# A hybrid attention block: other latencies in the hand-made order of the tensor engine, and a gate tile in the first head

## The chip, the core and the metric

The kernel runs on one core of a Trainium2 chip. Its engines work side by side, each from its own queue of instructions and in the order of that queue: TensorE (PE in the rows, PEld for its weight loads), VectorE (DVE), ScalarE (ACT), GpSimd (POOL) and SyncE (SP), which here only issues DMAs. The metric is the time of one execution in device microseconds (us), smaller is better; the kernel before takes 1390.83 us, the median of three runs from 1388.82 to 1392.7.

## What is computed

One layer on 512 tokens of width 1024, all in float32. Shortened from the reference:

```python
u = rmsnorm(h, pre_mix_norm)
proj = u @ w_in                       # q, k, v of attention; qkv, z, b, a of the delta rule; 2 gates
o_a = diff_attention(da_q, da_k, da_v, ...)          # 8 heads, softmax1 - lam * softmax2
qkv = silu(causal_depthwise_conv(gdn_qkv, conv_w))
g_q, g_k = l2norm(...), l2norm(...)                  # 8 heads, each for 2 value heads
o_b = gated_delta_rule(g_q, g_k, g_v, log_decay, beta)
o_b = rmsnorm(o_b) * silu(gdn_z)
merged = sigmoid(gate_a) * (o_a @ w_branch_a) + sigmoid(gate_b) * (o_b @ w_branch_b)
h = h + rmsnorm(merged @ w_out)
h = h + rmsnorm(square(relu(rmsnorm(h) @ w_up)) @ w_down)
h = h + rmsnorm((p @ w_ple) * sigmoid(h @ w_ple_gate))
```

The delta rule works on chunks: a triangular matrix is inverted for each chunk, and then a state is carried from chunk to chunk.

## The kernel before

Every large product is a "dense tile": 128 output channels by 512 tokens, with weights and activations split into a high and a low part, so three matmuls for each 128 rows of the weights. A tile of the input projection is 24 matmuls of 128x512 (`dense_steps`); `fill` yields after each pair of them.

Between the prologue and the branch products lies the scheduled section, in which the input projection (filler, in the order of `units`) and the work of the eight heads (chains) share TensorE. A head h has six chains, each a generator that emits a step and then yields:

- A (`gdn_a`): transposes and squares of keys and queries (psk, psq), the products of keys and queries (psx), and the transposed values (psv). One PSUM buffer, tag "a".
- I (`gdn_i`): the inverse of the 16x16 blocks, on VectorE (tiles L, Uq, tmpq), with DMAs through DRAM (ld_d, ud_d) ahead of it and behind it.
- U (`gdn_u`): the inverse is widened to the full block in matmul steps: psY16, psU16, psY, psT and psU, ps6, ps7.
- S (`gdn_s`): the states. For each of four chunks: psS (from the state's halves Sh and Sl), X, psV, vs and vn, psN and psO, and the new state.
- N (done mark "B", `gdn_n`): the norm of the delta rule's output, the transposes psoT, the product zs, and its store to ob_d.
- T (`attn`): differential attention, four blocks of 128 queries: psat (scores), softmax to aw, psaT (transposes), aT, psao, and at the end psaoT.

U, S and N take their PSUM buffers from one pool with two buffers (pool pb, tag "b"), which go round in the order of allocation: an allocation waits until the reader of the one before the last has finished.

What a generator yields is the assumed latency: the number of us of TensorE work that shall stand between this step and the chain's next. `run` keeps a clock that adds the estimated time of the emitted matmuls and nothing else. It emits the first chain in the list whose due time has come, otherwise the next filler pair; with neither it would let the clock jump. So the yields fix the order of TensorE's queue when the program is built. The other engines' queues are ordered by the framework's scheduler by priority (`URGENT`). What is on a queue waits for what stands ahead of it. A chain starts when the marks it names are done: U of head h waits for U of head h-1, A for A of h-1, and so on. After the last head's tiles 16 branch gate tiles follow as filler (`branch_gate`: tanh to gth, stored to g_d).

The names in rows are the program's, with the buffer numbers left out, so psY and psY16 both read psY, and ps6 and ps7 both ps. All matmuls of helper `mm` have line 80.

Of the kernel before, what the change touches and what calls it, by code (L numbers as in the profile page):

```python
# [37 lines left out]
def hybrid_block(ctx, tc, xT, pT, w1, wba, wa, wb, wo, wup, wdn, wple, wpg, vecs, rows, consts, out):  # L38
# [276 lines left out]
    done = set()  # L315
# [202 lines left out]
    def gdn_u(hk):  # L518

        B, U = (st_[hk][n] for n in "BU")  # L520
        Bf = B.rearrange("p i c n -> p (i c) n")
        U4 = U.rearrange("p e (k n) -> p e k n", k=4)
        bq = b0, b1, b2, b3 = [slice(32 * i, 32 * i + 32) for i in range(4)]
        yield 18.0

        T16 = [TT[:, :, 0], TA[:, :, 1], TT[:, :, 1], T3]
        for i in range(4):
            V.transpose(T16[i][bq[i]], U4[bq[i], :, i])
        Y16 = [Ye[:, :, 0], Yx[:, :, 0, :16], Ye[:, :, 1], Yx[:, :, 1, :16]]
        yield 6.0  # L530
        psY16 = pb.tile([128, 8, 16], F32, name="psY16", tag="b")
        for e in range(8):
            for i in range(4):
                mm(psY16[bq[i], e], Bf[:, e, bq[i]], T16[i][:, e, :16])
        for i in range(4):
            if i % 2:
                S.activation(Y16[i][bq[i]], psY16[bq[i]], AF.Copy, scale=nm16[bq[i]])
            else:
                V.tensor_scalar(Y16[i][bq[i]], psY16[bq[i]], nm16[bq[i]], None, op0=mult)
        yield 2.0  # L540
        psU16 = pb.tile([128, 8, 16], F32, name="psU16", tag="b")
        for e in range(8):
            for i in range(4):
                mm(psU16[32 * i:32 * i + 16, e], Y16[i][:, e], U4[:, e, i, 16:])
        for i in range(4):
            (S.copy if i % 2 else V.tensor_copy)(U4[32 * i:32 * i + 16, :, i, 16:], psU16[32 * i:32 * i + 16])
        yield 2.0
        V.transpose(TT[b0, :, 0], U4[b0, :, 0])
        V.transpose(TT[b2, :, 1], U4[b2, :, 2])
        V.transpose(TA[b1, :, 1], U4[b1, :, 1])  # L550
        V.tensor_copy(TA[b0, :, 0], TT[b0, :, 0])
        yield 5.0
        psY = pb.tile([128, 8, 32], F32, name="psY", tag="b")
        for e in range(8):
            mm(psY[b1, e], Bf[:, e, b1], TT[:, e, 0])
            mm(psY[b3, e], Bf[:, e, b3], TT[:, e, 1])
        V.tensor_scalar(Yx[b1, :, 0], psY[b1], -1.0, None, op0=mult)
        S.activation(Yx[b3, :, 1], psY[b3], AF.Copy, scale=-1.0)
        yield 2.0
        psT = pb.tile([128, 8, 32], F32, name="psT", tag="b")  # L560
        for e in range(8):
            mm(psT[b1, e], U[:, e, b1], Yx[:, e, 0])
        V.tensor_copy(TA[b1, :, 0], psT[b1])
        psU = pb.tile([128, 8, 32], F32, name="psU", tag="b")
        for e in range(8):
            mm(psU[b0, e], Yx[:, e, 0], U4[:, e, 1])
            mm(psU[b2, e], Yx[:, e, 1], U4[:, e, 3])
        S.copy(U4[b0, :, 1], psU[b0])
        V.tensor_copy(U4[b2, :, 3], psU[b2])
        yield 2.0  # L570
        ps6 = pb.tile([128, 8, 64], F32, name="ps6", tag="b")
        for e in range(8):
            mm(ps6[64:, e], Bf[:, e, 64:], TA[:, e])
        done.add(("B_read", hk))
        S.activation(Y6[64:], ps6[64:], AF.Copy, scale=-1.0)
        yield 2.0
        ps7 = pb.tile([64, 8, 64], F32, name="ps7", tag="b")
        for e in range(8):
            mm(ps7[:, e], Y6[:, e], U[:, e, 64:128])
        V.tensor_copy(U[:64, :, 64:128], ps7)  # L580
        yield 2.0

    def gdn_s(hk):

# [5 lines left out]
        for c in range(NC):  # L590
            c0 = c * 128
            if c:
                psS = pb.tile([128, 2, 2, 128], F32, name="psS", tag="b")
                ch = slice(c0, c0 + 128)
                for n in range(2):
                    mm(psS[:, n], kqh[:, n, ch], Sh, stop=False)
                    mm(psS[:, n], kql[:, n, ch], Sh, start=False, stop=False)
                    mm(psS[:, n], kqh[:, n, ch], Sl, start=False)
                X = bp.tile([128, 2, 128], F32, name="X")
                qs = bp.tile([128, 2, 128], F32, name="qs")  # L600
                for i in range(2):
                    hv = 2 * hk + i
                    V.scalar_tensor_tensor(X[:, i], in0=psS[:, 0, i], scalar=nbeg[:, c, hv:hv + 1], in1=vb[:, i, c], op0=mult, op1=add)
                for i in range(2):
                    hv = 2 * hk + i
                    S.activation(qs[:, i], psS[:, 1, i], AF.Identity, scale=eg[:, c, hv:hv + 1])
                xs = X
                yield 2.5
            else:
                xs = vb[:, :, 0]  # L610
            psV = pb.tile([128, 2, 128], F32, name="psV", tag="b")
            for i in range(2):
                mm(psV[:, i], U[:, 4 * i + c], xs[:, i])
            if c < NC - 1:
                vs = bp.tile([128, 2, 128], F32, name="vs")
                for i in range(2):
                    V.tensor_scalar(vs[:, i], psV[:, i], edr[:, i, c:c + 1], None, op0=mult)
            vn = bp.tile([128, 2, 128], F32, name="vn")
            S.activation(vn, psV, AF.Identity, scale=r2[:, c:c + 1])
            yield 2.5  # L620
            if c < NC - 1:
                psN = pb.tile([128, 2, 128], F32, name="psN", tag="b")
                mm(psN, kt[:, c], vs)
                Sn = bp.tile([128, 2, 128], F32, name="Sn", bufs=2)
                if c:
                    for i in range(2):
                        hv = 2 * hk + i
                        V.scalar_tensor_tensor(Sn[:, i], in0=St[:, i], scalar=egl[:, c, hv:hv + 1], in1=psN[:, i], op0=mult, op1=add)
                else:
                    V.tensor_copy(Sn, psN)  # L630
                St = Sn
                Sh, Sl = (bp.tile([128, 2, 128], F32R, name=f"S{n}") for n in "hl")
                split(Sh, Sl, St)
            psO = pb.tile([128, 2, 128], F32, name="psO", tag="b")
            for i in range(2):
                mm(psO[:, i], intra[:, i, c], vn[:, i])
            for i in range(2):
                if c:
                    V.tensor_tensor(o[i][:, c], psO[:, i], qs[:, i], op=add)
                else:  # L640
                    V.tensor_copy(o[i][:, c], psO[:, i])
                junk = bp.tile([128, 128], F32, name="bjunk")
                S.activation(junk, o[i][:, c], AF.Square, accum_out=sso[:, i, c:c + 1])
            if c < NC - 1:
                yield 3.0

    def gdn_n(hk):

# [4 lines left out]
        rsqrt(bp, rt.rearrange("p a c -> p (a c)"), sso.rearrange("p a c -> p (a c)"), 2 * NC)  # L653
        for i in range(2):
            V.tensor_tensor(o[i], o[i], bc(rt[:, i], [128, NC, 128], 2), op=mult)
        yield 11.0
        for i in range(2):
            zs = d["zs", i]
            psoT = pb.tile([128, T], F32, name="psoT", tag="b")
# [35 lines left out]
    def attn(h):  # L695
# [13 lines left out]
        for b in range(NC):  # L709
# [18 lines left out]
            V.scalar_tensor_tensor(rr, in0=rr, scalar=st[:, 2:3], in1=nlam, op0=mult, op1=mult)  # L728
            V.tensor_scalar(l2[:, b:b + 1], st[:, 2:3], st[:, 2:3], EPS, op0=mult, op1=mult)
            V.scalar_tensor_tensor(ws[0][:, :n], in0=ws[1][:, :n], scalar=rr, in1=ws[0][:, :n], op0=mult, op1=add)  # L730
            yield 6.0 + 0.5 * b
            psa = pt.tile([128, NC, 128], F32, name="psaT", tag="t")
            for kb in range(b + 1):
                transpose(psa[:, kb], ws[0][:, kb * 128:(kb + 1) * 128])
            aT = apool.tile([128, NC, 128], F32, name="aT", bufs=2)
            S.copy(aT[:, :b + 1], psa[:, :b + 1])
            yield 1.5
            pso = pt.tile([128, 128], F32, name="psao", tag="t")
            for kb in range(b + 1):
                mm(pso, aT[:, kb], vt[:, kb], start=kb == 0, stop=kb == b)  # L740
# [24 lines left out]
    def units():  # L765
        for h in range(-1, 8):
# [6 lines left out]
            if h >= 0:  # L773
                yield gate_tile(h, 0)
                yield gate_tile(h, 1)
            if h < 7:
                yield ak_tile(h + 1)
                yield av_tile(h + 1)
        for n in range(16):
            yield branch_gate(n)  # L780

    done |= {(n, -1) for n in ("kq_read", "B_read", "k_read", "av_read", "B", "T", "A", "I", "U")} | {("B_read", -2)}
    done |= {("v_read", -1, i) for i in range(2)} | {(n, -2) for n in "BT"}
    for h in range(8):
        chains.append([0.0, (("Z", h, 1), ("S", h)), gdn_n, h, ("B", h)])
        chains.append([0.0, (("U", h), ("B", h - 1)), gdn_s, h, ("S", h)])
        chains.append([0.0, (("I", h), ("U", h - 1)), gdn_u, h, ("U", h)])
        chains.append([0.0, (("av", h), ("T", h - 1)), attn, h, ("T", h)])
        chains.append([0.0, (("V", h, 1), ("A", h - 1)), gdn_a, h, ("A", h)])
        chains.append([0.0, (("A", h), ("I", h - 1)), gdn_i, h, ("I", h)])  # L790
    manual = tc.manual_schedule(engines={PE.engine})
    manual.__enter__()
# [308 lines left out]
```

## Time and profile before

| | |
|---|---|
| median of 3 runs | 1390.83 us |
| the profiled execution | 1397.38 us, its span 1395.6 us |
| TensorE busy | 1326.7 us (95% of the span), 8402 matmuls |
| VectorE, ScalarE, GpSimd busy | 838.1, 662.3, 184.5 us |
| mean granted TensorE clock | 0.98 of full |

"Idle before" is the time in which the engine did nothing ahead of an instruction, and the name behind the arrow is what ended it. PEclk is the granted clock of TensorE as a share of full speed. A row of waits gives the total in us, how often, and the longest.

### The profile page before, as it was taken

The numbers are of one execution on the slowest core, as the hardware profiler recorded it, in microseconds if no ns is written. First come the engines' busy times: TensorE is split into PE (matmuls) and PEld (weight loads), VectorE is DVE, ScalarE is ACT, GpSimd is POOL, SyncE is SP. The second block draws the span as 40 slices with busy tenths as digits, with TensorE's granted clock in tenths as the row PEclk, the third lists the DMA queues.
The fourth block names the chain that finished last, engine by engine and source line by source line (L and its number), as shares of the span: only waits on it lengthen the run. The fifth ranks groups of instructions, "written<-read, shape, count | busy, mean of one in ns | idle before, by whom it ended". The sixth has DMA issues, their size and how long they took to land.

```text
span 1395.6 us, 22459 instructions
## 1 busy us (share of the span) xinstructions
PE 1326.7 (95%) x8402; PEld 1107.5 (79%) x8402; DVE 838.1 (60%) x2155; ACT 662.3 (47%) x1363; POOL 184.5 (13%) x193
## 2 busy tenths in 40 slices
PE   6989999999999999999999999999999999999986
PEld 4867787787777778878888888898888888888985
DVE  6867688777778768776653534368343224433575
ACT  5556575767667476766453412254232223223241
POOL 3111111101111111110000000003320002210341
PEclk9989999999999999999999999999999999999998
DMA  7466655655665566655354743351232233223321
GB/s 249 134 153 132 154 122 135 157 150 126 162 158 139 134 134 166 149 135 143 117 185 167 249 143 113 101 186 46 67 100 91 91 94 102 91 91 108 112 84 61
DMA packets 91117, 182.58 MB, mean 131 GB/s; under 512 B 33632, under 2 KB 40160, under 8 KB 91008
## 3 DMA queue, kind: packets, MB, share of 16 engines
q1 hardware_dynamic: 81648, 147.07, 33.6%
q0 software_dynamic: 9360, 34.08, 13.2%
q8 instruction: 66, 1.08, 0.3%
q14 instruction: 43, 0.35, 0.1%
HBM read 130.19 MB, written 16.84 MB: 105 GB/s over the span
## 4 chain that ended last, share of the span: by engine, by line
PE 73%; DVE 14%; DMA 6%; ACT 3%; SPq 2%; issue 2%; POOL 0%; DVEq 0%; ACTq 0%; POOLq 0%
PE ps L80 64%; DMA dt<-gcr_d 2%; DVE Uq L507 1%; SPq L474 1%; PE psat L80 1%; DVE tmpq L506 1%; DVE h L881 1%; PE psao L80 1%; DMA L<-ld_d 1%; DVE ht L880 1%; DVE acc L372 1%; DMA U<-ud_d 1%; PE psS L80 1%; PE psx L80 1%; DVE nw_t L93 1%
## 5 line engine op out<-in xcount | busy, mean ns | idle before, releaser
L80 PE MATMUL ps<-u_hi,whi 128*128 128x512 f32 (+1 forms) x952 | 385.0, 405 | 0.0
L80 PE MATMUL ps<-u_lo,whi 128*128 128x512 f32 (+1 forms) x952 | 374.8, 395 | 0.0
L80 PE MATMUL ps<-u_hi,wlo 128*128 128x512 f32 (+1 forms) x952 | 250.1, 396 | 0.0
L98 ACT CAST whi<-raw 128x1024 fp32r<-128x1024 f32 (+1 forms) x116 | 116.4, 1005 | 265.4 <-PE ps L80 258.5
L80 PEld LDWEIGHTS ps<-u_hi,whi 128*128 128x128 f32 x952 | 183.2, 192 | 35.4
L80 PEld LDWEIGHTS ps<-u_lo,whi 128*128 128x128 f32 x952 | 183.4, 193 | 33.9
L99 DVE TENSOR_TENSOR wlo<-raw,whi 128x1024 fp32r<-128x1024 f32 x106 | 130.1, 1227 | 126.5 <-PE ps L80 104.2
L80 PEld LDWEIGHTS ps<-u_hi,wlo 128*128 128x128 f32 x952 | 172.6, 189 | 33.7 <-issue 0.2
L117 POOL DMA_DIRECT2D wlo<-raw x65 | 56.2, 864 | 424.5 <-ACT wlo L116 224.6
L80 PE MATMUL ps<-hid_hi,whi 128*128 128x512 f32 x224 | 88.5, 395 | 0.0
L80 PE MATMUL ps<-hid_lo,whi 128*128 128x512 f32 x224 | 88.4, 394 | 0.0
L80 PE MATMUL ps<-brl,whi 128*128 128x512 f32 x208 | 82.1, 394 | 0.0
L80 PE MATMUL ps<-brh,whi 128*128 128x512 f32 x208 | 82.0, 395 | 0.0
L372 DVE SCALAR_TENSOR_TENSOR acc<-ps,cw,acc 128x511 f32<-128x511 f32 (+2 forms) x96 | 71.3, 743 | 8.5 <-ACT acc L369 7.7
L115 ACT CAST whi<-raw 128x1024 fp32r<-128x1024 f32 x65 | 68.0, 1046 | 17.3 <-PE ps L80 17.0
L116 ACT ACTIVATE wlo<-whi 128x1024 fp32r<-128x1024 f32 x65 | 68.6, 1056 | 0.3
L942 POOL TENSOR_TENSOR mr<-mr 128x512 f32<-128x512 f32 (+1 forms) x37 | 39.5, 1070 | 217.9 <-ACT hid_hi L941 217.2
L940 DVE SCALAR_TENSOR_TENSOR mr<-ps,r 128x512 f32<-128x512 f32 (+1 forms) x37 | 22.9, 619 | 74.4 <-PE ps L80 70.7
L80 PE MATMUL ps<-hid_hi,wlo 128*128 128x512 f32 x224 | 56.9, 395 | 0.0
L80 PE MATMUL ps<-brh,wlo 128*128 128x512 f32 x208 | 52.6, 395 | 0.0
L80 PEld LDWEIGHTS ps<-hid_lo,whi 128*128 128x128 f32 x224 | 42.1, 188 | 10.3
L80 PEld LDWEIGHTS ps<-hid_hi,wlo 128*128 128x128 f32 x224 | 42.0, 188 | 10.2
(334 smaller groups left out, 2425.4 us busy)
## 6 DMA issues: line engine op xcount, KB each, us to landing
raw<-w SPq DMA_DIRECT2D x88, 512.0 KB, 3.5
wlo<-raw POOLq DMA_DIRECT2D x65, 512.0 KB, 4.8
raw<-wup SPq DMA_DIRECT2D x32, 512.0 KB, 3.3
raw<-wdn SPq DMA_DIRECT2D x32, 512.0 KB, 3.6
raw<-wb SPq DMA_DIRECT2D x16, 512.0 KB, 3.9
dt<-gcr_d SPq DMA_DIRECT2D x16, 256.0 KB, 5.1
bB<-ber_d SPq DMA_DIRECT2D x16, 256.0 KB, 5.2
ob_d<-zs SPq DMA_DIRECT2D x16, 256.0 KB, 3.0
```

The source lines that it names most:

```text
L80: PE.matmul(ps, lhsT=lhsT, rhs=rhs, start=start, stop=stop, **k)
L93: V.tensor_tensor(t, t, h, op=mult)
L98: S.copy(hi, src)
L99: (eng or V).tensor_tensor(lo, src, hi.bitcast(F32), op=sub)
L115: S.copy(whi, raw)
L116: S.activation(wlo, whi.bitcast(F32), AF.Copy, scale=-1.0)
L117: nc.gpsimd.dma_start(wlo, raw, accum_op=add)
L372: V.scalar_tensor_tensor(acc[:, s:], in0=ps[:, :T - s], scalar=cw[:, j, w:w + 1], in1=acc[:, s:], op0=mult, op1=add)
L474: nc.sync.dma_start(dst, Bf[bs, :, bs])
L506: V.tensor_tensor(tv, bc(L[:, j, j + 1:], [128, m, r], 1), bc(Uq[:, :m, j], [128, m, r], 2), op=mult)
L940: V.scalar_tensor_tensor(r[:, :n], in0=ps[:, :n], scalar=0.0, in1=r2[:, sl], op0=mx, op1=mult)
L942: G.tensor_tensor(r[:, :n], r[:, :n], r[:, :n], op=mult)
```

## The change

Three things change, all in the order of the scheduled section.

1. Assumed latencies: in U the yields behind psY16, psU16, psY, psT with psU, ps6 and ps7 go from 2.0 to 3.0. In S the yield behind psS goes from 2.5 to 3.0, the one behind psV from 2.5 to 3.5, and the one at the end of a chunk from 3.0 to 3.5. In N 11.0 becomes 12.0. In T the softmax's 6.0 + 0.5b becomes 7.0 + 0.5b, and the copy of aT 1.5 becomes 2.5.
2. Branch gate 0 moves from the end of the filler to a place behind head 0's two z gates.
3. A of head h also waits until S of head h-2 is done.

```diff
@@ gdn_u (six yields alike)
-        yield 2.0
+        yield 3.0
@@ gdn_s, behind psV
-            yield 2.5
+            yield 3.5
@@ units
+            if h == 0:
+                yield branch_gate(0)
             if h < 7:
                 yield ak_tile(h + 1)
                 yield av_tile(h + 1)
-        for n in range(16):
+        for n in range(1, 16):
             yield branch_gate(n)
@@ marks and chains
-    done |= {("v_read", -1, i) for i in range(2)} | {(n, -2) for n in "BT"}
+    done |= {("v_read", -1, i) for i in range(2)} | {(n, -2) for n in "BTS"} | {("S", -1)}
-        chains.append([0.0, (("V", h, 1), ("A", h - 1)), gdn_a, h, ("A", h)])
+        chains.append([0.0, (("V", h, 1), ("A", h - 1), ("S", h - 2)), gdn_a, h, ("A", h)])
```

Three places show what this does to the queues. The first is TensorE in the first softmax block of head 0, where psaT is the transpose of the softmax's output aw and psao the product that reads its copy aT; whi and wlo are the weights of filler tiles. The rows with - are before, those with + now.

```order
-L80 MATMUL ps<-u_hi,wlo_866 128x512 x2
+L80 MATMUL ps<-u_hi,wlo_866 128x512 x8
 L80 MATMUL psaT<-C,aw 128x128
-L80 MATMUL ps<-u_hi,wlo_866 128x512 x6
-L80 MATMUL ps<-u_hi,whi_947 128x512
-L80 MATMUL ps<-u_lo,whi_947 128x512
-L80 MATMUL psao<-vt,aT 128x128
```

psaT now stands six filler matmuls later. psao, the last row taken away here, stands twelve filler matmuls behind psaT where it stood eight behind it: ten more than before from the queue's common point.

The second place is ScalarE in head 1's A chain and head 0's third softmax block, before; the squares of psq (junk) are what psx waits for, and aw is the softmax's exponential, which waits for VectorE's maximum st.

```order
L420 COPY kt<-psk 128x512
L373 ACTIVATE vraw_1128<-acc 128x512
L115 CAST whi_1261<-raw_1259 128x1024
L721 ACTIVATE aw,st<-psat,st 128x384 x2
L413 ACTIVATE junk,gss<-psq 128x128
L674 ACTIVATE q_1253<-ps 64x512
```

The same place now:

```order
L420 COPY kt<-psk 128x512
L373 ACTIVATE vraw_1123<-acc 128x512
L115 CAST whi_1241<-raw_1239 128x1024
L743 ACTIVATE ajunk,asso<-oo 128x128
L413 ACTIVATE junk,gss<-psq 128x128 x3
L674 ACTIVATE q_1233<-ps 64x512
L413 ACTIVATE junk,gss<-psq 128x128
L116 ACTIVATE wlo_1242<-whi_1241 128x1024
L674 ACTIVATE q_1234<-ps 64x512
L721 ACTIVATE aw,st<-psat,st 128x384 x2
```

The squares of psq now stand ahead of the softmax's exponentials, and not behind them.

The third place is TensorE at head 1's step psT with psU of the U chain, before; both take a buffer of pool pb.

```order
L80 MATMUL psv<-C,vraw_1955 128x128 x4
L80 MATMUL psT<-Yx,U_349 32x32 x8
L80 MATMUL psU<-U_349,Yx 32x32 x16
L80 MATMUL psaT<-C,aw 128x128 x4
L80 MATMUL ps<-u_hi,wlo_2080 128x512 x6
```

The same place now:

```order
L80 MATMUL ps<-u_hi,whi_2188 128x512
L80 MATMUL ps<-u_lo,whi_2188 128x512
L80 MATMUL psO<-vn,intra 128x128 x2
L80 MATMUL psT<-Yx,U_349 32x32 x8
L80 MATMUL psU<-U_349,Yx 32x32 x16
L80 MATMUL psat<-k_1598,q_1233 128x512
```

psO of head 0's last chunk, also of pool pb, has come to stand straight ahead of psT and psU; psU takes the buffer that psO has just filled.

## Rows read from the trace of the kernel before

**Rows 1.** Stages: length, busy us (instructions) of five engines, granted clock, DMA share, GB/s.
```profile
70.00:665.00 595.00, 562.82 (x4339) 465.06 (x4338) 444.59 (x1434) 384.00 (x895) 83.58 (x86) 0.97 0.61 144
665.00:770.00 105.00, 105.00 (x724) 87.34 (x724) 52.42 (x118) 45.98 (x92) 0.00 (x0) 1.00 0.47 158
```

**Rows 2.** TensorE's waits, 35 to 775 us: total, times, longest.
```profile
PE psV L80 <- DVE X L603: 4.0, 5, 1.1
PE psao L80 <- ACT aT L736: 3.5, 1, 3.5
PE psx L80 <- ACT junk L413: 3.0, 1, 3.0
PE psN L80 <- DVE vs L617: 2.8, 2, 2.3
PE psoT L80 <- DVE zs L662: 2.6, 2, 1.5
PE psN L80 <- DVE tmpq L506: 2.5, 1, 2.5
PE psT L80 <- DVE Yx L557: 2.3, 1, 2.3
PE psaT L80 <- DVE aw L730: 2.1, 1, 2.1
PE psx L80 <- DVE l L729: 1.9, 1, 1.9
PE psS L80 <- ACT Sh L98: 1.6, 2, 1.0
PE psU L80 <- ACT Yx L537: 1.4, 4, 0.8
PE psO L80 <- ACT vn L619: 1.0, 2, 0.8
PE psY L80 <- DVE Sn L628: 0.9, 1, 0.9
PE psoT L80 <- ACT U L546: 0.6, 1, 0.6
...
PE ps L80 <- DVE zs L662: 0.5, 1, 0.5
```

**Rows 3.** Stretches of half clock, first and last of seven; columns as in Rows 1.
```profile
94.10:104.20 10.10, 6.63 (x17) 4.80 (x16) 8.50 (x25) 5.22 (x10) 2.57 (x3) 0.50 0.58 160
...
496.80:500.20 3.40, 3.40 (x12) 2.81 (x10) 2.83 (x9) 2.28 (x7) 0.86 (x1) 0.50 0.84 213
```

**Rows 4.** TensorE in time, at full and at half clock: start, us, instruction.
```profile
66.65 0.39 PE L80 MATMUL ps<-u_hi,whi 128*128 128x512 f32 x1
66.88 0.39 PE L80 MATMUL ps<-u_lo,whi 128*128 128x512 f32 x1
...
94.57 0.63 PE L80 MATMUL ps<-u_hi,whi 128*128 128x512 f32 x1
95.00 0.63 PE L80 MATMUL ps<-u_lo,whi 128*128 128x512 f32 x1
```

**Rows 5.** VectorE and ScalarE in time, three places: columns as Rows 4, then idle before.
```profile
90.22 0.36 DVE L431 SCALAR_TENSOR_TENSOR dt<-dt,gc_t,C 128x128 f32<-128x128 f32 x1 [4.71 <-DMA dt<-gcr_d]
...
98.79 0.26 ACT L736 COPY aT<-psaT 128x128 f32<-128x128 f32 x1
98.95 0.62 ACT L98 CAST kqh<-kq 128x512 fp32r<-128x512 f32 x1
...
121.93 0.43 DVE L528 STREAM_TRANSPOSE TT<-U 32x256 f32<-32x256 f32 x1 [2.80 <-DMA U<-ud_d]
```

**Rows 6.** The branch products and reloads: ns min/median/max, first and last start.
```profile
L80 PE MATMUL ps<-brh,whi x208: 390/394/404, 769.5 to 912.4; 128*128 128x512 f32 x104
L99 DVE TENSOR_TENSOR brl<-ot,brh x12: 1211/1226/1226, 719.9 to 799.8; 128x1024 fp32r<-128x1024 f32 x12
```

**Rows 7.** VectorE's waits for the dt tiles, 70 to 770 us: columns as in Rows 2.
```profile
DVE dt L431 <- DMA dt<-gcr_d: 15.4, 8, 4.7
```

More of the change, by code (lines that the diff above doesn't have):

```diff
@@ L546, in gdn_u @@
             (S.copy if i % 2 else V.tensor_copy)(U4[32 * i:32 * i + 16, :, i, 16:], psU16[32 * i:32 * i + 16])
-        yield 2.0
+        yield 3.0
         V.transpose(TT[b0, :, 0], U4[b0, :, 0])
@@ L558, in gdn_u @@
         S.activation(Yx[b3, :, 1], psY[b3], AF.Copy, scale=-1.0)
-        yield 2.0
+        yield 3.0
         psT = pb.tile([128, 8, 32], F32, name="psT", tag="b")
@@ L569, in gdn_u @@
         V.tensor_copy(U4[b2, :, 3], psU[b2])
-        yield 2.0
+        yield 3.0
         ps6 = pb.tile([128, 8, 64], F32, name="ps6", tag="b")
@@ L575, in gdn_u @@
         S.activation(Y6[64:], ps6[64:], AF.Copy, scale=-1.0)
-        yield 2.0
+        yield 3.0
         ps7 = pb.tile([64, 8, 64], F32, name="ps7", tag="b")
@@ L580, in gdn_u @@
         V.tensor_copy(U[:64, :, 64:128], ps7)
-        yield 2.0
+        yield 3.0
     def gdn_s(hk):
@@ L607, in gdn_s @@
                 xs = X
-                yield 2.5
+                yield 3.0
             else:
@@ L619, in gdn_s @@
             S.activation(vn, psV, AF.Identity, scale=r2[:, c:c + 1])
-            yield 2.5
+            yield 3.5
             if c < NC - 1:
@@ L644, in gdn_s @@
             if c < NC - 1:
-                yield 3.0
+                yield 3.5
     def gdn_n(hk):
@@ L655, in gdn_n @@
             V.tensor_tensor(o[i], o[i], bc(rt[:, i], [128, NC, 128], 2), op=mult)
-        yield 11.0
+        yield 12.0
         for i in range(2):
@@ L730, in attn @@
             V.scalar_tensor_tensor(ws[0][:, :n], in0=ws[1][:, :n], scalar=rr, in1=ws[0][:, :n], op0=mult, op1=add)
-            yield 6.0 + 0.5 * b
+            yield 7.0 + 0.5 * b
             psa = pt.tile([128, NC, 128], F32, name="psaT", tag="t")
@@ L736, in attn @@
             S.copy(aT[:, :b + 1], psa[:, :b + 1])
-            yield 1.5
+            yield 2.5
             pso = pt.tile([128, 128], F32, name="psao", tag="t")
```

## The prediction

> **What bounds the kernel now.** I read the stages first. TensorE has no free time from 665 to 770 us, and the change ends there; what it can touch is the stretch from 70 to 665 us, where TensorE is busy 562.8 of 595.0 us at a mean clock of 0.97 [rows 1]. So 32.2 us of idle time is the first pot. The second is the clock: seven stretches stand at half of full speed (1.2 and not 2.4 GHz), one of 10.1 us and six of about 3.4 us [rows 3]. There two matmuls of 512 columns start 0.43 us apart and not 0.23 [rows 4], so a stretch loses about half its length, 1.6 us for a short one and 5 us for the long one. Both pots together hold some 45 us; work that TensorE does is not changed at all, 8 heads and 16 gates in either order.
>
> The waits of TensorE tell who fills the first pot [rows 2]. They come in four kinds, and the sum below goes by them: (a) psaT and psao in the first softmax block, 2.1 + 3.5 = 5.6 us; (b) steps whose assumed latency is raised, psV, psN, psO, psS, psU and psT, together 15.6 us; (c) steps that found no free buffer of the two in pool pb, psoT behind zs and U, psY behind Sn and ps7 behind zs, 2.6 + 0.6 + 0.9 + 0.5 = 4.6 us; (d) the A chain, above all psx with 3.0 and 1.9 us, whose latencies stay.
>
> **The change part by part.**
>
> (a) The long wait of the first head. VectorE sat idle 4.71 us at dt, whose DMA landed at 90.2 us [rows 5]; aw is queued behind it. In the new order the rows of VectorE between these softmax scores and aw are the same, so aw comes at the same time. psaT stands six matmuls later: 6 x 0.23 = 1.4 us of its 2.1 are covered. psao is reached after another 12 x 0.23 = 2.8 us, at about 95.7, but what it waits for is aT, copied at 98.79 by a ScalarE that was held by the second dt; and now the cast kqh (0.62 us) stands ahead of aT and no longer behind it [rows 5]. So psao starts near 99.7 and waits 4.0. New sum 0.7 + 4.0 against 5.6: gain 0.8, and the long stretch of half clock stays. Bounds: nothing, and 2.4 if the extra ten matmuls count whole.
>
> (b) Raised latencies. A wait shrinks by what the latency grows, no more. psV gets 0.5 us in each of five waits: 2.5. psN gets 1.0: of 2.3 it covers 1.0, of the other 0.5 all, of the 2.5 again 1.0, so 2.5. psO is in the same step as psN, and I give it 0.7 of its 1.0. psS: twice 0.5. psU behind Yx, four waits of at most 0.8: all 1.4. psT: 1.0 of 2.3. Sum 9.1 of 15.6 [rows 2]. Bounds: 15.6 if the waits spread out when the chains do, 3 if the long ones return elsewhere.
>
> (c) Buffers of pool pb. I counted in both orders how much TensorE work stands between the last matmul into a buffer and the next one that takes it. Before, four allocations have 0.45 us (one psoT, or one psN, between), and these are the four waits of 0.9, 0.5, 1.5 and 1.1, on average 1.0; a fifth with 1.8 us waited 0.6 for the slower copies of U. Now U and S of neighbouring heads overlap more, and six allocations have 0.45 us, three have 0.9, two 1.35, like psU behind psO at the third place shown. At the same time to empty a buffer (0.45 + 1.0) they wait 6 x 1.0 + 3 x 0.55 + 2 x 0.1 = 7.9 us. Against 4.6 that is a loss of 3.3. Bounds: no loss, and 11 x 1.5 - 4.6 = 12 if each costs as much as the worst.
>
> (d) The A chain. The psx wait of 3.0 stood behind the exponentials of a softmax block, and these behind a VectorE that waited 2.80 us for U [rows 5]; in the new order the squares that psx needs are ahead of the exponentials, so this wait goes. Against it A of heads 2 to 7 now starts right where S of two heads before ends, with N's products and often U's and T's steps beside it, and its own latencies have not grown. The trace has no such pile; the nearest rows are the two psx waits, so between 0 and 6 x 3.0 = 18. I take 2.0, near what the eight heads show now, since ScalarE and VectorE are busy 65 and 75% of this stretch [rows 1]. Net gain 1.0.
>
> (e) The moved gate: 24 matmuls x 0.23 = 5.5 us, done earlier. Its DMA, ScalarE cast and VectorE split (1.2 us, as a split of this size [rows 6]) lie beside the fill of head 1; uncovered they would cost these 1.2. The last head ends later: its last psoT now stands 18 filler matmuls, some 4 us, ahead of the section's end. The reload of ob_d comes behind it; its last split began at 799.8, while the eight products that don't need it start at 769.5 and take 8 x 24 x 0.23 = 44 us, to 813. That cover of 12 us holds [rows 6]. Cost nothing.
>
> (f) The clock. The six short stretches follow waits of 3.0, 2.3, 1.9, 2.5, 1.5 and 2.3 us; no wait of up to 1.1 us has one behind it [rows 2]. The first goes, three others come down to 1.3 or 1.5, where the trace is silent. I take 2.5 of six, 2.5 x 1.6 = 4.0. Bounds: none, and all six, 9.6.
>
> Sum: 0.8 + 9.1 - 3.3 + 1.0 + 4.0 = 11.6 us less. The profiled execution, 1397.4 us (its span 1395.6, so 1.8 lie around it), would come to 1385.8; it lies 6.6 above the median, so by the median 1390.8 - 11.6 = 1379 us.
>
> **The rivals.**
>
> Slower, through the buffers. The longer plan makes U, S and N ask for pool pb close behind each other, and the chain that is stopped stops TensorE with it. Without (c) the sum is a gain of 14.9, and eleven close allocations eat it from (14.9 + 4.6) / 11 = 1.8 us each. With the worst wait seen, 1.5, and the clock falling behind every second one (0.8), each costs 2.3: 25.3 - 4.6 - 14.9 = 5.8 slower, 1397 us. For it speaks that these waits are new in kind at psO, psV and psU; against it that only one of the four now has a half clock behind it. The Trainium skill, Perfetto Trace Analysis, section Optimization Strategy, says that the same gap over and over on the engine that should be full can mean that PSUM has no room for the next tile; by that rule a longer latency buys nothing. The trace agrees for 4.6 of 32.2 us.
>
> No difference. The longest waits come from an engine that is held by something that has not landed: VectorE waited eight times for dt, 15.4 us in all [rows 7], with the chains' products behind it. Then a latency of 1 us more only moves which step is hit. The three long waits of (b), 2.5, 2.3 and 2.3, give nothing (3.0 of my 9.1), A's new waits eat the 3.0 of psx, and no stretch of half clock goes: 0.8 + 6.1 - 3.3 = 3.6, so 1387 us. The Trainium skill, PSUM — Partial Sum Buffer, section Engine vs sequencer instructions, says that the queues of ScalarE and VectorE are strictly first in, first out, which is the ground for this case; the trace agrees, with aw behind dt at 90.2 us.
>
> More than forecast. The waits are linked: a TensorE that does not stop keeps the others fed evenly. Then pool pb costs no more than now, both psx waits go (4.9) and so do all six short stretches: 0.8 + 9.1 + 4.9 + 9.6 = 24.4, 1366 us.
>
> The section's end is late. Were the last head's ob_d later than its 12 us of cover, the change would not do what it should; 1399 us at 20 us of overrun. The second product over it begins only behind 44 us, which speaks against.
>
> **How the numbers follow.** Forecast 0.45, more 0.22, no difference 0.17, slower by buffers 0.13, late end 0.03. About 0.3%, 4.2 us, is what a measurement of this kernel can tell from no change. The forecast's own range is 1373 to 1385, all faster by more than that, save a small tail that I give to the same. So faster 0.66, the same 0.18, slower 0.16. For 8 in 10 the range must hold most of "more" and of "slower": 1364 to 1397.
>
> **What would show it.** In the trace after: psaT and psao near 92 and 99 us still wait 4 to 5 us together; psT, psS, psN and psV wait for VectorE under 8 us in total; waits of psO, psU, psV and psoT behind zs, Sn, o or U copies, some 8 us; fewer than five short stretches of half clock; TensorE idle about 25 us from 70 to 665 us. Wrong would be: idle time of 32 us or more, with waits of A's steps at the heads' starts, or waits of pool pb above 15 us.

## The result, and the profile after

The changed kernel is slower: 1408.27 us (median of 4, 1407.09 to 1410.63) against 1391.76 (median of 4), ratio 1.0110, 95% interval 1.0086 to 1.0134. The forecast was 1379 us in a range of 1364 to 1397. The profiled execution took 1407.36 us, its span is 1405.6.

The two stages of the kernel after, columns as in [rows 1]:

```profile
70.00:665.00 595.00, 549.41 (x4262) 452.88 (x4260) 429.21 (x1384) 372.48 (x858) 83.63 (x86) 0.98 0.60 144
665.00:770.00 105.00, 104.99 (x744) 87.72 (x743) 62.81 (x164) 52.09 (x125) 0.00 (x0) 1.00 0.41 136
```

TensorE's idle time from 70 to 665 us rose from 32.2 to 595.0 - 549.4 = 45.6 us; the clock is slightly better. The first branch product, which marks the end of the scheduled section, starts at 781.1 us and not at 769.5 [rows 6]: 11.6 us later, while the span grew by 10.0, so all of what these two executions differ by arises in this section, and 13.4 us more idle time are enough for it. By the medians the loss is 16.5 us: the profiled execution before lay 5.6 us above its median and the one after 0.9 below, so the rows account for 10.0.

TensorE's waits in the kernel after, columns as in [rows 2]:

```profile
PE psat L80 <- ACT vt L704: 17.2, 6, 4.5
PE psao L80 <- ACT aT L736: 7.2, 3, 4.2
PE psT L80 <- DVE Yx L557: 5.1, 3, 3.0
PE psO L80 <- DVE Sn L628: 2.5, 3, 0.9
PE psx L80 <- DVE intra L466: 2.0, 2, 1.7
...
PE psv L80 <- DVE intra L466: 1.2, 1, 1.2
PE psV L80 <- DVE zs L662: 1.2, 2, 0.8
...
PE psS L80 <- ACT Sh L98: 0.8, 1, 0.8
PE psaT L80 <- DVE aw L730: 0.8, 1, 0.8
...
PE psY L80 <- DVE zs L662: 0.6, 1, 0.6
PE psx L80 <- ACT junk L413: 0.6, 1, 0.6
...
PE psV L80 <- DVE X L603: 0.3, 1, 0.3
```

The first row is new: psat waits for vt, 17.2 us in six waits, and no row of [rows 2] is like it. All other idle time from 70 to 665 us comes to 45.6 - 17.2 = 28.4 us, less than the 32.2 before.

What vt itself waits for stands in ScalarE's waits of the kernel after:

```profile
ACT vt L704 <- DMA oa_d<-of: 18.0, 6, 6.3
```

One of the six, in time order, all engines, columns as in [rows 5]; head 0's T ends with `of`, and head 1's T begins:

```profile
163.01 0.69 ACT L755 ACTIVATE of<-psaoT,gsub 128x512 f32<-128x512 f32 x1
163.73 0.34 SPq L756 DMA_DIRECT2D oa_d<-of  x1
...
164.64 0.60 PE L80 MATMUL psav<-C,vT 128*128 128x128 f32 x4
...
170.97 0.58 ACT L704 COPY vt<-psav 128x512 f32<-128x512 f32 x1 [5.08 <-DMA oa_d<-of]
...
171.60 0.38 PE L80 MATMUL psat<-k,q 128*128 128x256 f32 x1 [3.93 <-ACT vt L704]
```

Read it from the top. ScalarE writes `of`, the output of head 0's attention, and SyncE issues its store. Tiles `of` (line 754) and vt (line 703) carry the same tag "vt" in a pool that keeps one buffer of it. So head 1's copy of psav into vt must wait until the store has landed, 7 us after its issue. ScalarE stands idle 5.08 us in front of this copy. psav in turn keeps one of the two PSUM buffers of pool pt. The first psat of the block took the other one at 167.28; the second needs psav's, and TensorE stops for 3.93 us.

Two of the six stretches of half clock, columns as in [rows 3]; the others, of 3.4 us each, begin at 172.2 (straight behind the wait just shown), 254.1, 329.2 and 503.3:

```profile
100.50:103.90 3.40, 3.40 (x9) 2.65 (x8) 3.33 (x9) 2.40 (x6) 2.20 (x2) 0.50 0.40 77
...
585.20:592.00 6.80, 4.70 (x14) 4.04 (x15) 6.27 (x27) 4.82 (x12) 1.27 (x1) 0.50 0.27 84
```

The reload at the end, as in [rows 6], and VectorE's waits for dt, as in [rows 7]:

```profile
L99 DVE TENSOR_TENSOR brl<-ot,brh x12: 1225/1226/1227, 741.6 to 811.6; 128x1024 fp32r<-128x1024 f32 x12
```

```profile
DVE dt L431 <- DMA dt<-gcr_d: 26.8, 11, 4.7
```

The last split began at 811.6, and TensorE needs it 44 us behind 781.1. The waits for dt, 15.4 us before, are 26.8 now.

### The profile page after: what moved, and what is told of

Read it like the earlier page. It is cut to its first block, busy times and chain, and to the rows that moved or that the text cites. A ratio compares the mean times of both kernels' runs of the same rounds, so it can differ in the third digit from the quotient of the medians.

```text
span 1405.6 us, 22461 instructions
## 1 busy us (share of the span) xinstructions
PE 1322.7 (94%) x8402; PEld 1103.2 (78%) x8402; DVE 838.0 (60%) x2155; ACT 660.0 (47%) x1363; POOL 184.2 (13%) x193
## 4 chain that ended last, share of the span: by engine, by line
PE 73%; DVE 13%; DMA 8%; SPq 2%; issue 2%; ACT 2%; POOL 0%; DVEq 0%; ACTq 0%; POOLq 0%
PE ps L80 63%; DMA oa_d<-of 2%; DMA dt<-gcr_d 1%; SPq L474 1%; PE psat L80 1%; DVE h L883 1%; PE psS L80 1%; PE psV L80 1%; PE psO L80 1%; DMA wlo<-raw 1%; DVE tmpq L506 1%; DMA L<-ld_d 1%; PE psao L80 1%; DVE ht L882 1%; DVE acc L372 1%
```

## The experiments

The change has four parts: T's latencies, those of U, those of S with N, and the gate with the condition on A. The raised U, or S with N, goes only with the condition; without it the queues of the kernel would wait for one another for ever. To these comes one edit of mine, called W below: the output tile of T goes to the buffers of aw (three, long free by then), so that vt shares its buffer with nothing that is stored. W leaves TensorE's queue word for word as it is. "Ratio" is always against the kernel before on the same chip, with its 95% interval.

**The store in front of vt.** Theory V says that the six waits for the store are the loss; its rival P puts it on pool pb and on A chains that pile up. First the changed kernel with W:

```diff
-        of = apool.tile([128, T], F32, name="of", tag="vt")
+        of = apool.tile([128, T], F32, name="of", tag="aw", bufs=3)
```

> The changed kernel with tile of in the ring of the aw tiles and no longer in the buffer of vt; order of TensorE unchanged. Theory V (the next head's vt waits on ScalarE for the store of of to land, and TensorE's psat behind it): the six waits of psat behind vt, 17.2 us, and the three to four stretches of half clock behind them (17 us long, so 8 us lost) go; 1408 - 25 = 1383 us, 1378 to 1390. Rival P (pool pb and the piled A chains make the loss, and a freed TensorE stops at the next of them): psat's waits go but others grow, 1400 us or more.

1395.19 us, ratio 1.0011 (0.9994 to 1.0028). One edit of a buffer takes back 13 of the 16 us, against P. It falls short of the 1383 that V expected. The edit is not quite alone: the framework now orders VectorE's queue otherwise at 78 of its 2155 rows and ScalarE's at 33 of 1363, counted from the two traces.

The control, W on the kernel before, in whose trace no copy of vt waits for a store:

> The kernel before with tile of in the ring of the aw tiles. Control: no instruction of it waits for the store in the trace of before, so theory V expects no difference, 1388 to 1394 us. If the ring of aw is itself of help or harm, it shows here.

1393.63 us, ratio 1.0002 (0.9988 to 1.0015): nothing, as it should be.

T's latencies alone on the kernel before, and then with W:

```diff
-            yield 6.0 + 0.5 * b
+            yield 7.0 + 0.5 * b
...
-            yield 1.5
+            yield 2.5
```

> The kernel before with T's two latencies raised alone. In the plan a head's T begins 0 to 3 us after the last one's end. Theory V: ScalarE waits for the store in most heads, psat 10 to 17 us, and with the clock 1400 to 1412 us, slower than before though U, S, N, the gate and A's condition are as before. Rival P: 1387 to 1394 us, as before.

> The kernel before with T's raised latencies and with T's output tile in the buffers of aw, so vt waits for no store. The kernel with T raised alone took 1394 us and had 6.7 us of psat waiting for vt, in four waits. Theory V (the store is a cost that stands by itself): these 6.7 us go, 1386 to 1390 us, faster than both kernels. Rival S (every new order of the queue brings new idle time of 33 to 45 us and some half clock, about as much as it takes away; the kernel before lies at the low end of this scatter): 1391 to 1400 us.

1394.05 us, ratio 1.0007 (0.9991 to 1.0023), and with W 1383.98, ratio 0.9930 (0.9912 to 0.9949), faster than both kernels. TensorE's wait in the kernel with T alone, then TensorE's first stage with W:

```profile
PE psat L80 <- ACT vt L704: 6.7, 4, 2.6
```

```profile
70.00:665.00 595.00, 572.91 (x4560) 473.31 (x4560) 459.22 (x1461) 391.71 (x913) 83.49 (x86) 0.99 0.61 148
```

Idle time falls to 22.1 us, though in an execution (1377.89 us) that lies 6.1 below its median. The wait was worth 6.7 us; the gain is 10, and here only 8 rows of VectorE's queue and 10 of ScalarE's stand elsewhere. V missed that T alone did not come out slower (its 1400 to 1412 us were to come from 10 to 17 us of waits), but as a cost that stands by itself the store is shown: W gives 10 us here, 13 in the changed kernel, and nothing where nothing waits for the store.

The reverse, the changed kernel with T's latencies back, without and with W:

> The changed kernel with the two latencies of attention (T) as before, 6.0 + 0.5b and 1.5; all else changed. In the plan a head's T then ends 5 to 13 us before the next one's begins, where the changed kernel has 0 to 3. Theory V: psat waits behind vt for under 3 us in all, 1385 us, 1379 to 1393. Rival P: the latencies of U, S and N and the new condition of A are left, so 1403 us or more.

> The changed kernel with T's latencies back and with the output tile of T in the buffers of aw, so vt needs no store to have landed. Theory V (the store costs wherever psat stands short behind it): the 5.7 us of psat's wait and the half clock behind them go, 1397 to 1401 us. Theory L: what stays, some 5 to 9 us above the kernel before, is that of U, S and N. Rival: no gain at all, 1404 us or more, because the idle time only moves.

1407.45 us (1.0095, 1.0065 to 1.0124) and 1408.33 (1.0090, 1.0054 to 1.0126). Without T's part the kernel is as slow as with it, and W does nothing. V fails in both, and the rivals' 1403 and 1404 us or more come true. TensorE's waits without W:

```profile
PE psao L80 <- ACT aT L736: 6.6, 6, 3.0
PE psat L80 <- ACT vt L704: 5.7, 2, 3.8
PE psx L80 <- DVE intra L466: 5.0, 2, 3.3
PE psS L80 <- ACT Sh L98: 3.9, 2, 2.1
```

psat's 5.7 us here are no store: no row of ScalarE's waits has vt behind a DMA in this kernel, its copy is only late in ScalarE's queue. The expectation for W had taken them for one. So the other parts cost as much by themselves, and that is a second cause.

**The other parts.** Theory L blames the latencies of U, S and N (close allocations of pool pb), C the condition on A, G the gate, S says that any new order brings its own idle time.

```diff
+            if h == 0:
+                yield branch_gate(0)
...
-        for n in range(16):
+        for n in range(1, 16):
...
-        chains.append([0.0, (("V", h, 1), ("A", h - 1)), gdn_a, h, ("A", h)])
+        chains.append([0.0, (("V", h, 1), ("A", h - 1), ("S", h - 2)), gdn_a, h, ("A", h)])
```

Gate and condition together, the gate alone, the condition alone:

> The kernel before with the moved branch gate and the condition that A waits for S of two heads before; all latencies as before. Theory L (the raised latencies of U, S and N do the rest of the damage, by close allocations of pool pb): no loss, 1388 to 1396 us; in its order only 4 pool allocations have under 1 us of cover, as before, and T of every head starts 6 to 14 us of planned TensorE work behind T of the head before, so no wait of psat for vt. Rival C (the condition or the gate does it, since A of a head is held and then piles on S and N): 1400 us or more, with waits of psx and psv.

> The kernel before with branch gate 0 moved into head 0, alone. The kernel with gate and condition, latencies as before, took 1407 us. Theory C (the condition on A does it): the gate is harmless, 1389 to 1395 us. Theory G (the gate does it): 1402 us or more. Rival S: anything from 1390 to 1408 us, with the idle time spread over waits that have nothing to do with the gate.

> The kernel before with the condition that A waits for S of two heads before, alone. Theory C: 1402 us or more, with waits of A's steps psx, psv, or of psU where U is piled on them. Theory G: 1389 to 1395 us. Rival S: anything from 1390 to 1408 us, its waits unlike those of the kernel with gate and condition.

1406.76 us (1.0084, 1.0055 to 1.0113), 1396.00 (1.0022, 1.0010 to 1.0034), 1398.98 (1.0051, 1.0031 to 1.0070). L fails: no latency is raised here, and the time is that of the kernel without T's part. Neither C's nor G's range is met: each part costs some of it, and the two add up to 0.73%, within the interval of the pair (0.84%, 0.55 to 1.13). The longest waits, of the three in this order:

```profile
PE psao L80 <- ACT aT L736: 8.5, 3, 4.3
PE psU L80 <- ACT Yx L537: 4.8, 7, 1.2
PE psU L80 <- DVE Ye L539: 3.8, 6, 1.3
```

```profile
PE psV L80 <- DVE X L603: 15.5, 7, 5.4
```

```profile
PE psV L80 <- DVE X L603: 8.5, 7, 2.3
PE psx L80 <- ACT junk L413: 3.6, 1, 3.6
```

psV's long waits of both single edits are not in the pair, which stops at psao and psU instead. So the times of the parts add up, and their waits do not. The latter is as S says, but S's range, 1390 to 1408 us, was too wide to fail.

Latencies of U, S and N with the condition, and T with gate and condition, without and with W:

> The kernel before with the raised latencies of U, S and N and the condition on A (without the condition this order deadlocks); T and the gate as before. 8 allocations of pool pb have under 1 us of cover against 4. Theory L: slower, 1400 to 1410 us, with psY, psU, psO, psV, psoT waits for buffers, 6 us or more. Rival C: as the kernel with the condition and the gate alone. If both are near 1392 us, what made the kernel slow is none of the parts alone but what the parts do together.

> The kernel before with T's raised latencies, the gate and the condition; U, S and N as before. T starts 0, 7.4, 0.5, 3.7, 0.5, 0.4, 1.4 us of planned work behind T of the head before. Theory L: near the kernel with T raised alone, 1392 to 1397 us, with psat waiting 4 to 8 us for vt. Rival C: 1400 us or more.

> T raised, gate moved, condition on A, as in the run that took 1399 us with psat waiting 8.2 us for vt, and T's output tile now in the buffers of aw. Theory V: 8.2 us less, 1389 to 1393 us. Rival S: no gain, 1396 to 1403 us, with other waits in place of psat's.

1407.29 us (1.0088, 1.0056 to 1.0121), 1398.87 (1.0033, 1.0016 to 1.0051), 1387.89 (0.9964, 0.9951 to 0.9978). The first run meets L's range and C's alike and decides nothing between them; of the 6 us of buffer waits that L asked for, its trace has 3.2 behind zs (psY 2.2, psV 1.0), and its longest waits are psao's 11.2 and psx's 7.3. The second falls between the ranges of L and C, with psat waiting 8.2 us for vt. In the third W gives 11 us once more, two more than V expected. And T's latencies, added to gate and condition, gain 8 us even without W.

**U against S and N.** In the changed kernel with W, U's latencies back to 2.0, or those of S and N back (2.5, 2.5, 3.0 and 11.0):

> The changed kernel with T's output tile in the buffers of aw (1395 us), and U's six yields back to 2.0. Theory U (U's later steps fall behind I's row and dt on VectorE, seen as psT waiting 7.9 us for Yx): these waits go, 1384 to 1389 us. Theory SN (the longer states meet the buffers, psO, psS): 1393 to 1397 us. 4 close pool allocations under 1 us, as in the kernel before.

> The same 1395 us kernel with the yields of S and N back. Theory U: nothing gained and psV's and psN's waits come back, 1394 to 1400 us. Theory SN: 1386 to 1390 us.

1387.06 us (0.9945, 0.9927 to 0.9964) and 1385.18 (0.9934, 0.9910 to 0.9958). Each theory is right where its own part is put back and wrong where the other's is: each half alone costs nothing against 0.9964 without either, and only both together come to 1.0011. The row in which they differ most, with both, then with U back, then with S and N back:

```profile
PE psT L80 <- DVE Yx L557: 7.9, 4, 3.0
```

```profile
PE psT L80 <- DVE Yx L557: 1.1, 1, 1.1
```

```profile
PE psT L80 <- DVE Yx L557: 0.7, 1, 0.7
```

Where one of these four waits comes from shows VectorE, in time, in the kernel with both; psY's last product had ended at 471.9:

```profile
476.08 0.61 DVE L431 SCALAR_TENSOR_TENSOR dt<-dt,gc_t,C 128x128 f32<-128x128 f32 x2 [4.39 <-DMA dt<-gcr_d]
476.73 0.42 DVE L557 TENSOR_SCALAR Yx<-psY 32x256 f32<-32x256 f32 x1
```

Yx is ready to run at 471.9, but it stands behind a dt whose DMA lands at 476.1. The other three stand behind other work of VectorE's queue, above all the row of small operations of I (lines 506 and 507), and at 637 us this row had itself been held, 4.88 us, for the DMA of L. The step that was given 1 us more has been moved into a hole of 4.4 us.

**dt loaded earlier.** Theory H: these held queues make the waits. The tiles dt and bB of the next head are allocated and their four loads issued (`load_dt`) at the end of A of the head before; TensorE's queue again stays word for word.

```diff
@@ gdn_a, start
+        if hk == 0:
+            load_dt(0)
+        dts, bds = dtb
-        dts = gpool.tile([128, 2, NC, 128], F32, name="dt")
-        bds = gpool.tile([128, 2, NC, 128], F32, name="bB")
...
-            nc.sync.dma_start(dts[:, i], gcr_d[hv:hv + 1, :]...
-            nc.sync.dma_start(bds[:, i], ber_d[hv:hv + 1, :]...
...
@@ gdn_a, end
+        if hk < 7:
+            load_dt(hk + 1)
```

On the kernel before, on gate and condition, on the changed kernel with W, on T with W:

> The kernel before with the loads of dt and bB for the next head issued at the end of A of the head before; TensorE's queue holds the same instructions in the same order. Theory H (VectorE and ScalarE, held by dt's landing, make TensorE's waits): most of VectorE's 15.4 us at dt go, save head 0's 4.7, and some 5 to 10 us of TensorE's idle time: 1380 to 1388 us. Rival O (the order and pool pb make them): 1390 to 1395 us.

> Gate and condition alone (1407 us) with the early loads of dt and bB. Theory H: gains 8 us or more, 1390 to 1399 us. Rival O: 1403 to 1408 us.

> The changed kernel with T's output tile in the buffers of aw (1395 us) and with the early loads of dt and bB. Theory H: the waits of psT for Yx behind dt go, 1384 to 1390 us, within 5 us of T raised alone with both. Rival O: 1393 to 1397 us.

> T raised alone with the output tile in the buffers of aw (1384 us) and with the early loads. Theory H: only 1.6 us of its TensorE idle time stood behind a DMA on VectorE, so little is left: 1379 to 1384 us. Rival O: the same or slower, 1383 to 1388 us.

1395.38 us (1.0015, 0.9999 to 1.0030), 1403.31 (1.0071, 1.0048 to 1.0094), 1400.81 (1.0044, 1.0029 to 1.0059), 1396.03 (1.0015, 1.0000 to 1.0030). By the ratios of their partners (1, 1.0084, 1.0011 and 0.9930) that is 2 us slower, 2 faster (both within the intervals), 5 slower and 12 slower. H's ranges are met nowhere. The edit didn't do what it was to do: VectorE's waits for dt in the first of them stayed, against 15.4 in [rows 7]:

```profile
DVE dt L440 <- DMA dt<-gcr_d: 17.6, 10, 2.5
```

The loads hardly came earlier. In the kernel before, a head's first load of dt is already issued 31 us (head 1) to 62 us ahead of psk, the first matmuls of its A, and in the first of these runs it moved by 3 us at most, not always forward. VectorE's operations on dt begin 24 to 55 us ahead of psk (heads 1 to 7), long before A needs them; moving these back was not tried. The last run tells more. Its TensorE order is that of the best kernel, and it lost all that one had gained. Its first stage and its longest wait:

```profile
70.00:665.00 595.00, 560.52 (x4351) 463.66 (x4350) 447.25 (x1437) 384.72 (x895) 83.46 (x86) 0.99 0.60 145
```

```profile
PE psV L80 <- DVE X L614: 5.6, 4, 3.3
```

Idle time is 34.5 us against 22.1. What the edit did change is SyncE's order: in the best kernel the loads of L for I went out behind the first load of dt (for head 1 at 135.0 us), and now they go out behind all four of dt and bB (at 138.6). VectorE's waits for L, in the best kernel and in this one, and one of these waits with TensorE's wait behind it:

```profile
DVE tmpq L506 <- DMA L<-ld_d: 7.3, 7, 2.8
```

```profile
DVE tmpq L517 <- DMA L<-ld_d: 21.1, 7, 6.0
```

```profile
314.97 0.17 DVE L517 TENSOR_TENSOR tmpq<-L,Uq 128x15 f32<-128x15 f32 x1 [4.36 <-DMA L<-ld_d]
...
318.60 0.60 DVE L628 TENSOR_SCALAR vs<-psV,edr 128x128 f32<-128x128 f32 x2
...
319.35 0.68 PE L80 MATMUL psN<-vs,kt 128*128 128x256 f32 x2 [3.45 <-DVE vs L628]
```

vs could have run at 313.2, when psV was done, but VectorE was held, and then worked off what stood ahead of vs. The waits of psaT (3.0 us at 96.1, with a hold for dt ahead as well), psY (1.7 at 151.4) and psV (3.3 at 476.1) follow a hold for L in the same way. The four come to 11.5 us; the idle time grew by 12.4. So the order of the other engines' queues is worth 12 us with not one instruction of TensorE moved, and H, whose ranges failed, has its mechanism here: TensorE waits behind a VectorE that is held by a DMA.

## Why the prediction was wrong

The first stage of reasoning held: the loss lies between 70 and 770 us, in idle time.

(a) The first block: forecast 0.7 + 4.0 us, measured psaT 0.8 and psao 4.2. Right. But the long stretch of half clock did not stay; it is 3.4 us and not 10.1.

(b) Here the forecast failed. The step said "A wait shrinks by what the latency grows, no more", and took each of the raised latencies, T's included (0.8 us, in (a)), only as cover for the wait of its own step. By the total it did well: psV (X), psN, psO (vn), psS, psU and psT should keep 6.5 us and keep 0.3 + 0 + 0 + 1.0 + 0.2 + 5.1 = 6.6. But that is luck: psV and psN should keep 1.5 and 2.8, and psT, which was to fall from 2.3 to 1.3, rose to 5.1 although its latency had grown. What the step left out is that a longer latency makes its chain end later. T of a head starts when the filler has made its av tile and T of the head before is done. By the planner's own clock, 1.3 to 14.3 us of TensorE work lay between T of one head and the next before; now it is 0 in six of seven places and 2.8 in the other. That is where vt meets the store. 17.2 us of waits are new by it, and W on this kernel gives 13 us back.

The same sentence failed a second time, more quietly. Without the store the changed kernel is at 1395 and not at the forecast 1379, because the savings are not a sum. T's latencies with W give 10 us, not 0.8. Gate and condition then cost about 5 of these (0.9930 to 0.9964), U's latencies or those of S and N nothing, and both together some 7 (0.9964 to 1.0011).

(c) Pool pb: forecast 7.9 us. Measured psO behind Sn 2.5, psV behind zs 1.2, psY behind zs 0.6, ps behind zs 0.4, so 4.7. The count of close allocations was right, their price too high. The rival that was to make the kernel slower by this pool got the sign right and the mechanism wrong. The rule quoted there from the Trainium skill (Perfetto Trace Analysis, Optimization Strategy) speaks of SBUF as well as PSUM, and I weighed it for PSUM alone: the buffer that was lacking is vt's, in SBUF, 17.2 us of the 45.6.

(d) A chain: forecast about 4.7 us left; measured psx 2.0 + 0.6, psv 1.2 and psq 1.1, 4.9. Right in size, and the psx wait of 3.0 behind junk went to 0.6, much as said. That gate and condition, by themselves, cost 12 us in another order was not seen: I priced the condition as waits of A's own steps, and in those runs the waits are psU's, psV's and psao's.

(e) The late end cost nothing: last split at 811.6, needed at 781.1 + 44 = 825.

(f) Clock: the half-clock time in this stretch fell from about 30.5 to 23.8 us, so 3.4 us against the forecast 4.0, with four of the six stretches now at waits of psat.

Put together: forecast 11.6 less, measured 11.6 more in the section. Of the 23.2 between them 17.2 are the wait for vt, 3.8 other idle time that shrank less than said (28.4 against 24.6), 0.6 the clock, and 1.6 are not accounted for. By the medians the forecast missed by 29 us, 1408 against 1379; the other 6 are mostly that it was counted from a profiled execution 6.6 above its median. The "no difference" rival, which was given 0.17, had one thing right: ScalarE and VectorE work in strict order (the rule it took from PSUM — Partial Sum Buffer, Engine vs sequencer instructions, in the Trainium skill), and the trace of the changed kernel with W agrees with it at 476.08, where Yx stood ready behind dt. I used it for dt and never asked what else in the diff makes a queue's head wait.

**What stays open.** Why gate and condition cost 12 us, and why U with S and N cost time together when each half costs nothing. Some of the new waits were followed back to a VectorE held by a DMA, above; the others were not. From 70 to 770 us VectorE's waits for DMAs come to 37 us before, 21 in the best kernel, 36 in the three others that are faster, 47 to 55 with gate, condition or both, and 61 with U, S, N and condition. So they go with the time in these orders, but that they make it is not shown, and against it two kernels at the time of before have 62 (the changed one with W) and 25 (T alone). A test that takes the hold away was not reached. That T's latencies gain 10 us is not explained by T's own waits either: in that kernel psao still waits 3.9 us (3.5 before), and it is the waits of psV, psN, psx and psT that shrink.

The best version is T's latencies alone with W: 1383.98 us, ratio 0.9930.

## What to carry to other kernels

When a planned latency grows, ask first what its chain's later end meets: the next user of each of its buffers, and above all buffers that are freed by a store's landing. A saving worked out wait by wait, with all else held fixed, is no bound in a kernel whose order a planner makes: here T's latencies, priced at 0.8 us, gave 10 with W, and two parts that cost nothing alone cost 7 us together. Before tuning latencies, take out shared buffers whose release hangs on a DMA, since an order that is slow with one (T alone, 1394) can be the fastest without it (1384). And look at operations that stand in a queue long before they are needed: if one waits for a DMA, all behind it wait too.

## What the runs showed of the hardware

A store of 256 KB (oa_d) took 2.0 to 4.2 us from issue to landing before, and 2.1 to 7.4 after: in these two kernels its landing was no constant that a planner could count on.

Like orders differ in half clock, and not in idle time alone: ahead of the first branch product the stretches at half clock add up to 31 us before, 24 after, 14 in the best kernel and 34 in the one with U, S, N and condition. If a stretch loses half its length, as by the starts in [rows 4], some 10 us lie between the last two.
